# Products of the gated mixer and the joining move from GpSimd to VectorE, reciprocal roots from VectorE to GpSimd, in a one-layer hybrid decoder

## The chip, the cores and the metric

One Trainium2 chip, one of its cores. The metric is the device time of one execution in microseconds; a kernel's time is the median of several runs.

The engines are named PE (TensorE, matrix products), PEld (its loading of the stationary operand), DVE (VectorE), ACT (ScalarE), POOL (GpSimd) and SP (the engine whose queue issues most DMAs). Each engine carries out its instructions in the order in which the program lists them.

## What is computed

One layer over 2048 prompt rows and 64 sample rows (8 sequences of 8), model width 1024:

```
h    = rms_norm(x, g_norm);  proj = h @ w_in           # 1024 -> 3584
u, va, za, q, k, vb, zb = split(proj)
q, k = rms_norm over 64 columns per head (8 heads)
# mixer A, 4 groups of 128 columns, chunks of 128 rows
vn    = rms_norm(va, g_va);  mixed = tril(w_s) @ vn + b_s
a_out = rms_norm(u * mixed, g_oa) * silu(za)
# mixer B: three dilated sliding windows (128/1, 512/4, 2048/16)
for each pattern: o_i, lse_i = softmax attention over its window
b_out = sum_i exp(lse_i) o_i / sum_i exp(lse_i)
b     = rms_norm(b_out, g_ob) * silu(zb)
h     = x + concat(a_out, b) @ w_out
y     = h + sigmoid(h @ w_ple_gate) * rms_norm(p @ w_ple, g_ple)
```

Further outputs are the normed keys, the values and, for the samples, the normed `va`. The samples attend to a cache of 2048 older keys and values.

## The kernel before

Products are made of 16-bit halves (high and low part of each operand, three products), so that every 128-row tile of a weight chunk takes 24 matrix products. The input projection is cut into eight weight chunks, four of kind A (u, va, za of one group, 384 columns) and four of kind B (q, k, vb, zb of two heads, 512 columns), in the order A0 B0 B1 A1 B2 B3 A2 A3. Each chunk runs over 16 prompt tiles and one sample tile; four tiles form a group.

- `xnorm`, `xhalves`, `xtrans` (from line 400) make the normed, split and transposed rows of a tile; the first chunk makes them on its way, so its first products wait for them.
- `b_evac` and `a_evac` copy a product out of PSUM. After each group `b_norm` (line 493) norms q and k, scales the gate and sends it off; `b_trans` splits q and k and has them transposed by DMA into the tile `qk`. `a_norm` (line 573) norms va, and `a_mix` (line 595), some time later, mixes with `w_s`, norms and gates.
- `scores` and `stage_c` are the attention: products into `pss`, maximum and mask on DVE (line 704), exponentials on ACT, split into halves on DVE (lines 715, 716), a DMA that transposes them (`pT`), and products with the values. The patterns' results go to DRAM.
- `combine` (line 755), 16 times, reads three patterns' results of 512 rows and two heads back (`rl`), weights and adds them, norms and gates (`gzl`), and writes to `catd`.
- In the last stage, 17 tiles, `p3_cat`, `p3_out`, `p3_h`, `p3_gate` and `p3_ple` (line 924) make the output products. The samples' attention (`sample`) is spread between them; it multiplies cached keys by queries on POOL (line 1126), and DVE adds these up (line 1127). POOL also adds the residual at the end of each tile (line 963).

`rsqrt` (line 179) is a starting value from the bits and two Newton-like corrections: eight DVE instructions on 1 to 16 columns (lines 183 to 190), called 115 times. Its argument `mul` folds a power of two into the last two steps.

What sets the order: a planner (`Pump`) puts units of attention between the products by costs in nanoseconds written in the code, and a scheduler with a timeline of its own then lays down each engine's list. The list is fixed when the kernel is built.

## Time and profile before

| | |
|---|---|
| median of 3 runs | 1526.22 us (1517.96 to 1528.44) |
| the profiled execution | 1526.24 us, its span 1524.5 us |
| mean granted TensorE clock | 0.959 |
| PE busy | 1361.5 us, 89% of the span, 8280 products |
| DVE busy | 1160.8 us, 76%, 3775 instructions |
| ACT busy | 725.9 us, 48%, 2083 instructions |
| POOL busy | 538.1 us, 35%, 547 instructions |

Busy time is that between start and end of an instruction as recorded; an instruction that started and was held up by something counts as busy. Idle time before an instruction is put down to what ended it. The sum over an engine says little by itself: a stretch in which PE idles and one in which it doesn't are to be read apart.

### The profile page before, as it was taken

To read this page: it belongs to the slowest core of one execution; us is meant where nothing else is said; L and a number is where in the kernel's file an instruction comes from. 1 tells how busy PE (TensorE), PEld (TensorE's weight loads), DVE (VectorE), ACT (ScalarE), POOL (GpSimd) and SP (SyncE) were. 2 spreads that over 40 slices of the span, in tenths; PEclk is the share of its full clock that TensorE was granted. 3 is DMA by queue.
4 is the path that set the end of the run, shared out by engine and by line. 5 is a ranking of instruction groups with operands and counts; after the bars stand their busy time and mean duration, and the time that the engine had idled before them with its cause. 6 is when DMAs were issued, how large, how long until landed. Compare 5 with 4: busy or idle time off the path is not lost. (4 is left out here: it accounts for less than half of the span.)

```text
span 1524.5 us, 26216 instructions
## 1 busy us (share of the span) xinstructions
PE 1361.5 (89%) x8280; PEld 693.3 (45%) x8280; DVE 1160.8 (76%) x3775; ACT 725.9 (48%) x2083; POOL 538.1 (35%) x547
## 2 busy tenths in 40 slices
PE   2989988997899988899888986788998999899998
PEld 1544544554555434455445643443343344344443
DVE  6777887588988789876999899879756675675555
ACT  6675666565656446655665544754322122221222
POOL 7123122234543654322344356643232330330101
PEclk9999999999999999999999998799999999999999
DMA  7983698588965457977697587876899799796432
GB/s 195 238 181 97 131 176 171 119 176 183 210 155 126 132 120 161 215 142 164 151 211 161 127 207 222 230 204 157 208 224 251 188 255 240 194 242 155 105 94 64
DMA packets 591436, 266.06 MB, mean 175 GB/s; under 512 B 338337, under 2 KB 568801, under 8 KB 591297
## 3 DMA queue, kind: packets, MB, share of 16 engines
q1 hardware_dynamic: 589312, 262.73, 75.4%
q0 software_dynamic: 1984, 1.66, 0.7%
q8 instruction: 65, 1.06, 0.3%
q14 instruction: 75, 0.61, 0.1%
HBM read 134.56 MB, written 48.01 MB: 120 GB/s over the span
## 5 line engine op out<-in xcount | busy, mean ns | idle before, releaser
L441 PE MATMUL psg<-wt,xT 128*128 128x512 f16 (+1 forms) x3072 | 649.6, 367 | 36.5 <-DVE agz L571 15.2
L441 PEld LDWEIGHTS <-xT 128*128 128x128 f16 x3072 | 309.9, 102 | 331.3 <-issue 60.1
L712 ACT ACTIVATE sm<-sm,rec,psc 128x256 f32<-128x256 f32 (+1 forms) x384 | 185.1, 546 | 129.4 <-DVE rec L708 103.1
L698 PE MATMUL pss<-qk 128*128 128x256 f16 (+1 forms) x384 | 132.0, 355 | 31.2 <-DMA qk<-qkc 17.2
L1126 POOL TENSOR_TENSOR K<-K,qB 96x512 f32<-96x512 f32 x64 | 88.4, 1386 | 165.8 <-DMA K<-in_cache_k_dram 70.3
L704 DVE CUSTOM_DVE_ANT_0 sm<-pss,mask 128x256 f32<-128x256 f32 (+1 forms) x384 | 122.7, 360 | 29.2 <-PE pss L699 28.1
L699 PE MATMUL pss<-qk 128*128 128x256 f16 (+1 forms) x384 | 132.8, 358 | 0.0
L874 PEld LDWEIGHTS <-Th 128*128 128x128 f16 x800 | 77.1, 99 | 109.9 <-issue 21.5
L874 PEld LDWEIGHTS <-Tc 128*128 128x128 f16 x800 | 76.4, 98 | 110.6 <-issue 19.9
L716 DVE TENSOR_TENSOR pc<-sm,pc 128x512 f16<-128x512 f32 (+1 forms) x160 | 119.0, 744 | 1.6
L963 POOL TENSOR_TENSOR tg<-tg,x 128x1024 f32<-128x1024 f32 (+1 forms) x16 | 37.6, 2347 | 183.4 <-DVE tg L962 160.4
L874 PE MATMUL psg<-w,Th 128*128 128x512 f16 x400 | 97.6, 387 | 1.2 <-DMA Th<-hl 0.5
L861 ACT ACTIVATE hl<-x,sm 128x1024 f16<-128x1024 f32 (+1 forms) x17 | 19.5, 1147 | 166.0 <-DVE sm L842 140.7
L715 DVE CAST pc<-sm 128x512 f16<-128x512 f32 (+1 forms) x160 | 80.5, 503 | 23.3 <-ACT sm L712 21.3
L874 PE MATMUL psg<-w,Tc 128*128 128x512 f16 x400 | 95.6, 379 | 2.8 <-DMA Tc<-hl 2.8
L874 PE MATMUL pss<-w,Th 128*128 128x512 f16 x400 | 94.9, 379 | 0.0
L874 PE MATMUL pss<-w,Tc 128*128 128x512 f16 x400 | 93.8, 379 | 0.0
L1127 DVE TENSOR_REDUCE blk<-K 96x8 f32<-96x512 f32 x64 | 43.0, 678 | 61.2 <-POOL K L1126 61.1
L776 POOL TENSOR_TENSOR rl<-rl,sm 128x520 f32<-128x520 f32 x48 | 55.7, 1187 | 82.9 <-ACT sm L772 80.0
L739 PEld LDWEIGHTS <-pT 128*128 128x128 f16 x600 | 57.3, 98 | 52.7 <-DMA pT<-pc 43.9
L513 POOL TENSOR_TENSOR gz<-gz,gch 128x512 f32<-128x512 f32 x16 | 20.8, 1301 | 168.9 <-DVE gz L491 83.9
L744 ACT ACTIVATE rec<-pso 128x130 f32<-128x130 f32 (+1 forms) x160 | 44.4, 295 | 46.7 <-PE pso L741 45.3
(324 smaller groups left out, 2649.5 us busy)
## 6 DMA issues: line engine op xcount, KB each, us to landing
K<-in_cache_k_dram SPq DMA_DIRECT2D x64, 192.0 KB
qB<-qd SPq DMA_DIRECT2D x64, 192.0 KB
V<-in_cache_v_dram SPq DMA_DIRECT2D x64, 192.0 KB
vt<-vscr SPq DMA_DIRECT2D x32, 258.0 KB
K<-in_cache_k_dram SPq DMA_DIRECT2D x32, 256.0 KB
V<-in_cache_v_dram SPq DMA_DIRECT2D x32, 256.0 KB
cat<-catd SPq DMA_DIRECT2D x16, 512.0 KB
x<-in_x_prompt_dram SPq DMA_DIRECT2D x16, 512.0 KB
```

Source lines behind the costliest of these rows:

```text
L441: last_mm[0] = nc.tensor.matmul(g[:, :ncol], lhsT=l, rhs=r, start=(n == 0), stop=(n == (23 if j < NT else 15)))
L698: nc.tensor.matmul(pss[:, s, h], lhsT=Q[:, h, qs], rhs=KH[:, h, ks], start=True, stop=False)
L699: nc.tensor.matmul(pss[:, s, h], lhsT=Q[:, h, qs], rhs=KL[:, h, ks], start=False, stop=True)
L704: nc.vector.tensor_tensor_reduce(sm4[:, s, h], pss[:, s, h], mk, 1.0, -3.0e38, op0=ALU.add, op1=ALU.max, accum_out=mx[:, i:i + 1])
L712: nc.scalar.activation(sm4[:, s, h], sm4[:, s, h], AF.Exp, bias=r[:, sl + s, h, HD + 1:HD + 2], scale=psc)
L715: nc.vector.tensor_copy(pc[:, :n], smv)
L716: nc.vector.tensor_tensor(pc[:, n:2 * n], smv, pc[:, :n], op=ALU.subtract)
L739: nc.tensor.matmul(po[:, s, h, 0:65], lhsT=H, rhs=v[:, vs_, a:a + 65], start=(bi == 0), stop=False)
L744: nc.scalar.activation(r[:, sl:sl + ns, :, 0:65], po[:, :ns, :, 0:65], AF.Copy)
L776: nc.gpsimd.tensor_tensor(ti, ti, e[:, i, :].unsqueeze(2).to_broadcast([P, 8, 65]), op=ALU.mult)
L874: last_mm[0] = nc.tensor.matmul(gs[hf], lhsT=o[part][:, kt], rhs=w[:, kt % 2, half, :], start=(n[hf] == 0), stop=(n[hf] == (3 if m == P el ...
L1126: nc.gpsimd.tensor_tensor(K3, K3, qB, op=ALU.mult)
```

## The change

Four things are done, and nothing else in the program text:

- `rsqrt` becomes one POOL instruction, a power with the exponent -0.5 out of a constant tile `mhalf`. The powers of two that were folded into the last steps move into the scale and the constant of the instruction ahead, for which `wprep` makes one more column of `sc` (1 DVE instruction in each of the eight chunks).
- In `b_norm`, `a_norm` and `a_mix` the products go from POOL to DVE. In `b_norm` the q half takes row factor and gain in one pass for each head; in `a_mix` the row factor and the gate are one pass for each tile of the group.
- In `combine` the first pattern is scaled on DVE, and the other two are scaled and added in one pass for each of 8 column blocks; the squares go to ACT; row factor and gate are one pass for each block.
- The residual add of the last stage and the key products of the samples stay on POOL.

```diff
-    def rsqrt(src, n, p=P, mul=1.0):
+    def rsqrt(src, n, p=P):
         y = small(n, f"rsy{n}")[:p]
...
-        nc.vector.scalar_tensor_tensor(y, t, 1.5 * 0.375 * mul, y, op0=ALU.add, op1=ALU.mult)
+        nc.gpsimd.tensor_tensor(y, src, mhalf[:p, :n], op=ALU.pow)
         return y
...
@@ b_norm
-        nc.gpsimd.tensor_tensor(rv, rv, y.unsqueeze(2).to_broadcast([m, 4 * n, HD]), op=ALU.mult)
...
-                nc.gpsimd.tensor_tensor(ko[:, q, :].rearrange("p (h d) -> p h d", d=HD), kv[:, q],
+                for h in range(2):
+                    nc.vector.scalar_tensor_tensor(qv[:, q, h], qv[:, q, h], y4[:, q, h:h + 1], gqk,
+                                                   op0=ALU.mult, op1=ALU.mult)
+                nc.vector.tensor_tensor(kv[:, q], kv[:, q], y4[:, q, 2:4].unsqueeze(2).to_broadcast([P, 2, HD]),
+                                        op=ALU.mult)
+                nc.vector.tensor_tensor(ko[:, q, :].rearrange("p (h d) -> p h d", d=HD), kv[:, q],
                                         gkS.unsqueeze(1).to_broadcast([P, 2, HD]), op=ALU.mult)
-                nc.gpsimd.tensor_tensor(qv[:, q], qv[:, q], gqk.unsqueeze(1).to_broadcast([P, 2, HD]), op=ALU.mult)
...
-        nc.gpsimd.tensor_tensor(gzv, gzv, gch[:m, 0, :].unsqueeze(1).to_broadcast([m, n, P]), op=ALU.mult)
+        nc.vector.tensor_tensor(gzv, gzv, gch[:m, 0, :].unsqueeze(1).to_broadcast([m, n, P]), op=ALU.mult)
@@ a_norm
-        nc.gpsimd.tensor_tensor(gz, gz, gch[:m, 0, :].unsqueeze(1).to_broadcast([m, n, P]), op=ALU.mult)
-        nc.gpsimd.tensor_tensor(va, va, y.unsqueeze(2).to_broadcast([m, n, P]), op=ALU.mult)
+        nc.vector.tensor_tensor(gz, gz, gch[:m, 0, :].unsqueeze(1).to_broadcast([m, n, P]), op=ALU.mult)
+        nc.vector.tensor_tensor(va, va, y.unsqueeze(2).to_broadcast([m, n, P]), op=ALU.mult)
@@ a_mix
-        nc.gpsimd.tensor_tensor(t, t, G["gz"][:m, :n, :], op=ALU.mult)
-        nc.gpsimd.tensor_tensor(t, t, y.unsqueeze(2).to_broadcast([m, n, P]), op=ALU.mult)
+        for q in range(n):
+            nc.vector.scalar_tensor_tensor(t[:, q], t[:, q], y[:, q:q + 1], G["gz"][:m, q, :], op0=ALU.mult, op1=ALU.mult)
@@ combine
-        for i in range(3):
-            ti = rr[i][:, :, 0:65]
-            nc.gpsimd.tensor_tensor(ti, ti, e[:, i, :].unsqueeze(2).to_broadcast([P, 8, 65]), op=ALU.mult)
+        nc.vector.tensor_tensor(t0, t0, e[:, 0, :].unsqueeze(2).to_broadcast([P, 8, 65]), op=ALU.mult)
         for i in (1, 2):
-            nc.gpsimd.tensor_tensor(t0, t0, rr[i][:, :, 0:65], op=ALU.add)
+            for a in range(8):
+                nc.vector.scalar_tensor_tensor(t0[:, a], rr[i][:, a, 0:65], e[:, i, a:a + 1], t0[:, a],
+                                               op0=ALU.mult, op1=ALU.add)
...
-        nc.gpsimd.tensor_tensor(sq, o, o, op=ALU.mult)
+        nc.scalar.activation(sq, o, AF.Square)
...
-        nc.gpsimd.tensor_tensor(o, o, y.unsqueeze(2).to_broadcast([P, 8, HD]), op=ALU.mult)
...
-        nc.gpsimd.tensor_tensor(g8, o, g8, op=ALU.mult)
+        for a in range(8):
+            nc.vector.scalar_tensor_tensor(g8[:, a], o[:, a], y[:, a:a + 1], g8[:, a], op0=ALU.mult, op1=ALU.mult)
```

The scheduler makes a new order of all engines from this. Lines of the kernel before and after differ by up to nine; a root is line 181 after. Three places show what moved.

First place, the norm of q and k of the last group of a B chunk. On DVE before, five of the eight steps of a root (lines 185 to 189) stand between the halving of probabilities (715, 716) of the attention:

```order
L185 TENSOR_TENSOR sm_4645<-sm_4645,sm_4642 128x16
L716 TENSOR_TENSOR pc_4580<-sm_4569,pc_4580 128x256
L186 SCALAR_TENSOR_TENSOR sm_4645<-sm_4645 128x16
L187 SCALAR_TENSOR_TENSOR sm_4644<-sm_4645,sm_4644 128x16
L188 TENSOR_TENSOR sm_4645<-sm_4644 128x16
L715 CAST pc_4597<-sm_4586 128x256
L189 SCALAR_TENSOR_TENSOR sm_4645<-sm_4645,sm_4642 128x16
```

After, DVE has the products of the norm there instead (500: q, 502: k), in the midst of maximum (705) and halving (716); the root itself is one row of POOL, whose list holds hardly anything else in this stretch (197 loads a gain):

```order
L705 ISA sm_4252,sm_4253<-pss_4251,mask 128x128
L705 ISA sm_4253 128x1
L716 CAST pc_4243<-sm_4232 128x512
L500 SCALAR_TENSOR_TENSOR raw_4073<-raw_4073,sm_4460,gqk 128x64 x2
L502 TENSOR_TENSOR raw_4073<-raw_4073,sm_4460 128x128
```

```order
L197 DMA gch_3614<-in_g_va_dram 128x128
L181 TENSOR_TENSOR sm_3262<-sm_3260,mhalf 128x16
L181 TENSOR_TENSOR sm_4003<-sm_4001,mhalf 128x16
L181 TENSOR_TENSOR sm_4460<-sm_4458,mhalf 128x16
L181 TENSOR_TENSOR sm_3818<-sm_3814,mhalf 128x8
```

The instruction that makes the power's input (`sm_4458`) stands 17 DVE instructions ahead of the first that reads its result (`sm_4460`).

Second place, the start of POOL's list: loads of gains, of `b_s` (`bsS`) and of pieces of `w_s` (`bd`). Before:

```order
L206 DMA gch_668<-in_g_ob_dram 128x128
L312 DMA bsS<-in_b_s_dram 8x4x1 x8
L317 DMA bd_91<-in_w_s_dram 8x8x1 x4
L292 AFFINE_SELECT w_322<-w_322 128x512
L317 DMA bd_91<-in_w_s_dram 8x8x1 x28
L581 TENSOR_TENSOR agz_331<-agz_331,gch_441 128x512
```

After, the roots of the first input tiles stand between these loads:

```order
L197 DMA gch_567<-in_g_ob_dram 128x128
L305 DMA bsS<-in_b_s_dram 8x4x1 x8
L310 DMA bd_93<-in_w_s_dram 8x8x1 x3
L181 TENSOR_TENSOR sm_158<-sm_155,mhalf 128x1
L285 AFFINE_SELECT w_277<-w_277 128x512
L310 DMA bd_93<-in_w_s_dram 8x8x1 x3
L181 TENSOR_TENSOR sm_185<-sm_182,mhalf 128x1
L310 DMA bd_93<-in_w_s_dram 8x8x1 x17
L181 TENSOR_TENSOR sm_233<-sm_230,mhalf 128x1
```

What was eight DVE instructions for each tile now has loads of constants ahead of it.

Third place, POOL in the last stage, a tile in whose time keys of the samples are multiplied. Before, key products (1126) and the residual add (963):

```order
L1126 TENSOR_TENSOR K_2845_15710<-K_2845_15710,qB_15712 96x512
L1126 TENSOR_TENSOR K_2847_15716<-K_2847_15716,qB_15718 96x512
L963 TENSOR_TENSOR tg_15787<-tg_15787,x_2419_13725 128x1024
L1126 TENSOR_TENSOR K_2851_15737<-K_2851_15737,qB_15739 96x512
L1126 TENSOR_TENSOR K_2853_15743<-K_2853_15743,qB_15745 96x512
L963 TENSOR_TENSOR tg_16079<-tg_16079,x_2380_13561 128x1024
```

After, with the tiles' roots (181):

```order
L1127 TENSOR_TENSOR K_2745_15342<-K_2745_15342,qB_15344 96x512
L964 TENSOR_TENSOR tg_15413<-tg_15413,x_2327_13430 128x1024
L1127 TENSOR_TENSOR K_2749_15363<-K_2749_15363,qB_15365 96x512
L181 TENSOR_TENSOR sm_15478<-sm_15474,mhalf 128x1
L1127 TENSOR_TENSOR K_2751_15369<-K_2751_15369,qB_15371 96x512
L964 TENSOR_TENSOR tg_15697<-tg_15697,x_2291_13288 128x1024
L181 TENSOR_TENSOR sm_15729<-sm_15725,mhalf 128x1
```

A tile's root follows the residual add of the tile ahead, in places with a key product between.

## Rows read from the trace of the kernel before

**Rows 1.** Stretches: us, busy time of each engine, granted clock, DMA share, GB/s.

```profile
0.00:1000.00 1000.00, 866.60 (x5828) 480.37 (x5829) 816.84 (x2902) 584.00 (x1754) 403.58 (x456) 0.95 0.75 170
1000.00:1360.00 360.00, 336.40 (x1663) 142.94 (x1663) 250.42 (x642) 100.74 (x249) 118.11 (x85) 0.98 0.93 215
```

**Rows 2.** Waits of PE: waiter, what ended it, us in total, times, longest.

```profile
PE pso L739 <- DMA pT<-pc: 32.1, 23, 4.3
PE pss L698 <- DMA qk<-qkc: 17.2, 8, 3.6
...
PE psg L441 <- DVE agz L571: 15.2, 6, 6.8
PE pss L698 <- DVE sm L704: 13.6, 16, 1.7
```

**Rows 3.** Groups of DVE: longest and shortest line of the root; busy us, mean ns.

```profile
L184 DVE TENSOR_TENSOR sm<-sm 128x1 f32<-128x1 f32 (+5 forms) x115 | 39.8, 350 | 1.6
...
L188 DVE TENSOR_TENSOR sm<-sm 128x1 f32<-128x1 f32 (+5 forms) x115 | 20.5, 181 | 1.7
```

**Rows 4.** Groups of DVE by form: the nearest to the products that it gets.

```profile
L1147 DVE SCALAR_TENSOR_TENSOR blk<-blk 128x64 f32<-128x64 f32 x4 | 0.9, 220 | 0.0
...
L491 DVE SCALAR_TENSOR_TENSOR gz<-th,psg 128x128 f32<-128x128 f32 x64 | 17.9, 280 | 3.2 <-ACT th L490 3.0
...
L1032 DVE TENSOR_TENSOR blk<-blk,sc 128x512 f32<-128x512 f32 x1 | 0.7, 687 | 0.0
```

**Rows 5.** Timeline at 509 us: start, duration, instruction, idle before it.

```profile
509.03 1.44 DVE L184 TENSOR_TENSOR sm<-sm 64x1 f32<-64x1 f32 x1
...
509.42 1.03 POOL L781 TENSOR_TENSOR rl<-rl 128x512 f32<-128x512 f32 x1
```

**Rows 6.** Groups of DVE, two by form, two by line.

```profile
L716 DVE TENSOR_TENSOR pc<-sm,pc 128x512 f16<-128x512 f32 x140 | 108.5, 775 | 1.4
...
L715 DVE CAST pc<-sm 128x512 f16<-128x512 f32 x140 | 71.6, 511 | 22.6 <-ACT sm L712 20.7 <-DMA pT<-pc 0.9 <-DMA kd<-sb 0.2
...
L708 DVE TENSOR_SCALAR rec<-sm,nsc 128x2 f32<-128x2 f32 (+1 forms) x160 | 54.5, 353 | 10.4 <-DMA r2d<-rec 5.9 <-DMA r3d<-rec 2.4 <-DMA r1d<-rec 1.7
...
L617 DVE TENSOR_SCALAR sm<-sm,sm 128x4 f32<-128x4 f32 (+1 forms) x20 | 19.5, 975 | 11.1 <-ACT ua L615 8.4 <-ACT sb L615 2.7
```

**Rows 7.** Timeline of DVE at 656 us.

```profile
656.34 0.22 DVE L708 TENSOR_SCALAR rec<-sm,nsc 128x2 f32<-128x2 f32 x1
656.47 0.42 DVE L715 CAST pc<-sm 128x512 f16<-128x512 f32 x1
656.92 0.69 DVE L716 TENSOR_TENSOR pc<-sm,pc 128x512 f16<-128x512 f32 x1
```

**Rows 8.** PE at 651 us, and the stretch behind it (columns of rows 1).

```profile
651.08 0.39 PE L698 MATMUL pss<-qk 128*128 128x256 f16 x1 [3.54 <-DMA qk<-qkc]
...
651.90:654.70 2.80, 2.80 (x9) 1.08 (x8) 2.55 (x12) 0.15 (x1) 0.00 (x0) 0.60 0.57 115
```

**Rows 9.** Groups of POOL: a small product, the shortest iota, the longest product.

```profile
L511 POOL TENSOR_TENSOR sb<-sb,gqS 64x128 f32<-64x128 f32 x4 | 1.8, 444 | 0.0
...
L1057 POOL IOTA blk<- 128x2 int32 x1 | 0.1, 129 | 0.5 <-DVE sc L1054 0.5
...
L963 POOL TENSOR_TENSOR tg<-tg,x 128x1024 f32<-128x1024 f32 (+1 forms) x16 | 37.6, 2347 | 183.4 <-DVE tg L962 160.4 <-DVE sm L184 21.1 <-DVE sm L937 1.9
```

**Rows 10.** Timeline of the start.

```profile
13.21 1.13 ACT L416 ACTIVATE xhl<-room,sm 128x1024 f16<-128x1024 f32 x1
...
13.82 1.62 POOL L312 DMA_DIRECT2D bsS<-in_b_s_dram  x3 [1.70 <-DMA gch<-in_g_oa_dram]
...
22.34 5.90 PE L441 MATMUL psg<-wt,xT 128*128 128x384 f16 x24 [4.58 <-DMA xT<-xhl]
```

**Rows 11.** Waits: POOL from 1060 to 1365 us; DVE over the span.

```profile
POOL K L1126 <- DMA K<-in_cache_k_dram: 66.2, 12, 22.3
...
DVE blk L1127 <- POOL K L1126: 61.1, 30, 7.7
```

More of the change, by code (lines that the diff above doesn't have):

```diff
@@ L213, in tile_hymba_gmlp_dilated_attn_step @@
     nc.scalar.activation(small(1), ones[:, 0:1], AF.Square)
+    mhalf = cst.tile([P, 16], F32, name="mhalf")
+    nc.gpsimd.memset(mhalf, -0.5)
     mask = cst.tile([P, 2, P], BF16, name="mask")
@@ L374, in wprep @@
         nc.vector.tensor_scalar(sc[:, 4:5], sc[:, 3:4], VS * VS, None, op0=ALU.mult)
+        nc.vector.tensor_scalar(sc[:, 5:6], sc[:, 3:4], 2.0 ** -24, None, op0=ALU.mult)
         yield 0.0
@@ L406, in xnorm @@
             xsq[j] = nc.scalar.activation(hl[:m, 1].bitcast(BF16), xt[:m], AF.Square, accum_out=s2[:m])
-            nc.vector.tensor_scalar(s2[:m], s2[:m], 1.0 / D, EPS, op0=ALU.mult, op1=ALU.add)
-            y = rsqrt(s2[:m], 1, m, XS)
+            nc.vector.tensor_scalar(s2[:m], s2[:m], XS ** -2 / D, XS ** -2 * EPS, op0=ALU.mult, op1=ALU.add)
+            y = rsqrt(s2[:m], 1, m)
         xhl[j] = hl, y
@@ L496, in b_norm @@
         ms = small(16, "bms", 2)
-        nc.vector.tensor_scalar(ms[:m, :4 * n], G["ss"][:m, :4 * n], 1.0 / HD, sc[:m, 3:4], op0=ALU.mult, op1=ALU.add)
-        y = rsqrt(ms[:m, :4 * n], 4 * n, m, 2.0 ** 12)
-        rv = G["raw"][:m, :n, :].rearrange("p j (a d) -> p (j a) d", d=HD)
-        nc.gpsimd.tensor_tensor(rv, rv, y.unsqueeze(2).to_broadcast([m, 4 * n, HD]), op=ALU.mult)
+        nc.vector.tensor_scalar(ms[:m, :4 * n], G["ss"][:m, :4 * n], 2.0 ** -24 / HD, sc[:m, 5:6], op0=ALU.mult, op1=ALU.add)
+        y = rsqrt(ms[:m, :4 * n], 4 * n, m)
+        y4 = y.rearrange("p (j a) -> p j a", a=4)
         kv = G["raw"][:m, :n, 128:256].rearrange("p j (h d) -> p j h d", d=HD)
@@ L505, in b_norm @@
             for q in range(n):
-                nc.gpsimd.tensor_tensor(ko[:, q, :].rearrange("p (h d) -> p h d", d=HD), kv[:, q],
+                for h in range(2):
[4 more added lines that the diff above has]
+                nc.vector.tensor_tensor(ko[:, q, :].rearrange("p (h d) -> p h d", d=HD), kv[:, q],
                                         gkS.unsqueeze(1).to_broadcast([P, 2, HD]), op=ALU.mult)
-                nc.gpsimd.tensor_tensor(qv[:, q], qv[:, q], gqk.unsqueeze(1).to_broadcast([P, 2, HD]), op=ALU.mult)
         else:
-            nc.gpsimd.tensor_tensor(kv[:, 0], kv[:, 0], gkS[:m].unsqueeze(1).to_broadcast([m, 2, HD]), op=ALU.mult)
-            nc.gpsimd.tensor_tensor(qv[:, 0], qv[:, 0], gqS[:m].unsqueeze(1).to_broadcast([m, 2, HD]), op=ALU.mult)
+            for h in range(2):
+                nc.vector.scalar_tensor_tensor(qv[:, 0, h], qv[:, 0, h], y4[:, 0, h:h + 1], gqS[:m],
+                                               op0=ALU.mult, op1=ALU.mult)
+                nc.vector.scalar_tensor_tensor(kv[:, 0, h], kv[:, 0, h], y4[:, 0, h + 2:h + 3], gkS[:m],
+                                               op0=ALU.mult, op1=ALU.mult)
         gzv = G["gz"][:m, :n, :]
-        nc.gpsimd.tensor_tensor(gzv, gzv, gch[:m, 0, :].unsqueeze(1).to_broadcast([m, n, P]), op=ALU.mult)
+        nc.vector.tensor_tensor(gzv, gzv, gch[:m, 0, :].unsqueeze(1).to_broadcast([m, n, P]), op=ALU.mult)
         if m == P:
@@ L937, in p3_ple @@
         nc.vector.tensor_tensor(ms[:m], s2[:m, 0:1], s2[:m, 1:2], op=ALU.add)
-        nc.vector.tensor_scalar(ms[:m], ms[:m], 1.0 / D, None, op0=ALU.mult)
-        nc.vector.scalar_tensor_tensor(ms[:m], ic[:m], EPS, ms[:m], op0=ALU.mult, op1=ALU.add)
-        y = rsqrt(ms[:m], 1, m, 0.5)
+        nc.vector.tensor_scalar(ms[:m], ms[:m], 4.0 / D, None, op0=ALU.mult)
+        nc.vector.scalar_tensor_tensor(ms[:m], ic[:m], 4.0 * EPS, ms[:m], op0=ALU.mult, op1=ALU.add)
+        y = rsqrt(ms[:m], 1, m)
         e = wk.tile([P, D], F32, name=nm("e"), tag="raw", bufs=2)
```

13 lines of the change are left out of this document (3 added, 10 removed).

## Prediction

> **What bounds the kernel now.** I read the stretches first, then TensorE's waits, then the groups of VectorE and GpSimd. In the first 1000 us [rows 1] TensorE is busy 866.6 us and idle 133.4; VectorE is busy 816.8, GpSimd 403.6, and the granted clock averages 0.95. In the next 360 us TensorE is busy 336.4, so 23.6 idle: that later stage is TensorE's own work, and nothing that VectorE saves there comes back as time. What can be won lies in the 133.4 us. The waits of TensorE [rows 2] name who ends them: the transposed probabilities pT 32.1 us, the transposed q and k halves 17.2, the gate evacuation of the mixer 15.2, the row maximum that frees score banks 13.6, together 78.1. The first two are put down to a DMA, but what each DMA carries (pc, qkc) is written by VectorE just before. So VectorE, with 183.2 us free in 1000, is what feeds TensorE late; ScalarE and the queue of SP stand beside it in the same chains.
>
> **What goes from VectorE.** A root is eight instructions, called 115 times. Its eight lines are eight groups, of which [rows 3] show the longest (39.8 us) and the shortest (20.5); the eight together are 228.0 us.
>
> **What comes to VectorE.** Durations [rows 4]: 0.220 us for a scaled product of 128x64, 0.280 for 128x128 (its second operand is in PSUM, the nearest row), 0.687 for a plain product of 128x512.
> - Norm of q and k, 16 groups: eight products of 64 columns, eight of 128, one of 512: 1.76 + 2.24 + 0.69 = 4.69, in all 75.0 us.
> - Mixer norm, 16 groups: two of 512, 22.0 us. Mixer end: four of 128, 17.9 us.
> - Joining, 16 times: one of 520 columns (taken as 0.687), 16 of 65 and eight of 64 (taken as 0.220): 5.97, in all 95.5 us.
> - The sample groups: 16 small q and k products, 8 plain gate and value products, 4 gate products and 4 joint ones at 0.22 to 0.28: 7.9 us.
>
> Sum 218.3, so VectorE's own work falls by 9.7 us only. The squares of the joining go to ScalarE, 16 instructions; that engine was busy 584.0 of 1000 [rows 1], which hides them; uncovered they would cost some 11 us (estimate: 16 at the 0.687 us of a 512-column product [rows 4]).
>
> **What VectorE gets back from GpSimd.** [rows 5] show the price of the old placing: a 64x1 step of the root took 1.44 us and ended with the GpSimd product that ran beside it (509.42 + 1.03). The same lengthening stands in the means [rows 6] against the same lines while GpSimd is quiet [rows 7]: the 512-column difference 775 against 690 ns, 140 times, 11.9 us; the cast 511 against 420, 140 times, 12.7; the bias 353 against 220, 160 times, 21.3; the mixer's mean square 975 against the same 220 for a short tensor-scalar, 20 times, 15.1. That is 61.0 us. Smaller groups are left uncounted, and the products of the sample keys and of the final sum stay on GpSimd, so the last stage keeps its collisions. VectorE in all: -9.7 - 61.0 = -70.7 us, nearly all of it in the first 1000 us: 746 busy, 254 free.
>
> **From VectorE to TensorE.** An instruction's wait in a line behind others grows roughly as busy over free time: 816.8/183.2 = 4.46 before, 746/254 = 2.94 after, a third less. I apply that third (34%) to the 78.1 us of [rows 2]: -26.6 us. The bounds are none of them (the chains may hang on DMA and ScalarE alone) and all of them, -78.1. The removed GpSimd steps themselves also shorten the way from the norm to the transposed q and k; this is in the same 17.2 us and not counted again.
>
> [...]
>
> **The power.** No row shows one. The nearest GpSimd instruction by shape [rows 9] is a 64x128 product at 0.444 us; the shortest, an iota of two elements, takes 0.129; the longest product 2.347. I take 0.444, near the low end because a root has 1 to 16 elements, and keep 0.129 to 2.347 for the range. The eight steps it replaces take 228.0/115 = 1.98 us, so at 0.444 the value comes sooner. In the built order 38 of the 115 powers have at most two VectorE instructions between the instruction that makes their input and the one that reads the result, and 15 have none; the other 77 are covered by attention's instructions. At 0.444 us no wait is left that counts.
>
> **The start.** GpSimd's queue is strict, and the first power now stands behind its eight small loads of b_s and three of w_s [second order place]. Those loads issue until 15.44 us, three more at 0.54 (1.62 us for three) end at 17.06 [rows 10], so the first root comes at about 17.5 us, where ScalarE used it at 13.21. The first transposed tile is then up to 4.3 us later, and TensorE began its first product at 22.34 having waited for just that. It idles again a few us later for the second tile, which takes up part: +2 us, bounds 0 and 4.3. [...]
>
> **The last stage.** There each tile's root stands behind a GpSimd product of the final sum, for some tiles behind products of sample keys too [third order place], and these wait for their loads: 66.2 us in 12 waits, the longest 22.3 [rows 11]. VectorE reads those products in its own strict order and waited 61.1 us for them already, while TensorE idled only 23.6 us in 360. I charge +5 us; bounds 0 and 23.6 (as much idling again).
>
> **Sum**, against the profiled 1526.24 us, which equals the median 1526.22: -26.6 - 10 + 2 + 5 = -29.6, so 1496.6, rounded 1497.
>
> **Rivals.**
> - *The waits stay.* 49.3 of the 78.1 us are written against DMAs, and a transposed DMA, its place in SP's queue and ScalarE's exponentials keep their length. A VectorE that is freer then waits itself. For it: the order is fixed in advance. Against it: 28.8 us are put down to VectorE directly. Nothing gained, +7: about 1526 with the start and the last stage partly hidden.
> - *The power is dear, the slow side.* One mechanism: VectorE, strict in order, stands at the reader of a root until GpSimd is done. The relief of 70.7 us is used up when the 115 roots cost 0.61 us of standing each; from there it turns. At 0.8 us each VectorE loses 92, is 21 us worse than before, at 838 of 1000; 838/162 = 5.17 is 16% above 4.46, so +12.5 on the waits, +5 on the clock, +7: 1551. For it: no row has the power, and 38 roots stand nearly bare. Against it: 1 to 16 elements, and 77 covered; the bare ones alone would need 1.9 us of standing each.
> - *The whole wait goes.* All 78.1 and 29 of the clock, +7: 1426. The order of all engines is made anew, which can help or hurt. For it only the size of the relief on GpSimd (403.6 us of 1000); against it the DMAs.
>
> **How the numbers follow.** Forecast 0.55 (its own range 1475 to 1513), waits stay 0.20, dear power 0.20, all gone 0.05. A measurement of this kernel can tell about 1% (15 us). Faster by more than that: most of the forecast, 0.51, and the last rival, 0.05: 0.56. Slower: the dear power and a part of the rest whose loss at the start or in the last stage reaches its bound, 0.24. The same: 0.20. The low end of the range takes two thirds of the four waits and their share of the clock, -52 - 20 + 2 + 5, 1461, and a little of the all-gone case: 1455. The high end takes most of the dear power: 1545.
>
> **What would show it.** Right: VectorE's busy time near 1090 us, its short lines at their quiet lengths (the bias near 220 ns), the four waits of TensorE near 52 us together, the granted clock of the first 1000 us at 0.96 or more, powers below 0.5 us each. Wrong: VectorE waiting for the power's line in its list of waits for tens of us; the four waits as before although VectorE is freer; a first product of TensorE later than 27 us; idle TensorE in the last stage.

## The result, and the profile after

The changed kernel takes 1534.57 us (median of 20 runs, 1526.64 to 1541.69), the kernel before 1524.22 us in the 20 runs beside it. The ratio is 1.0071, 95% interval 1.0054 to 1.0089: 10 us slower, not 29 us faster. Its profiled execution has a span of 1532.7 us and a mean granted clock of 0.942 (before: 1524.5 us, 0.959).

The busy times of the page: VectorE fell by 100.7 us, GpSimd by 220.8, TensorE is within 5 us of where it was (1365.9 against 1361.5).

```profile
PE 1365.9 (89%) x8280; PEld 695.6 (45%) x8280; DVE 1060.1 (69%) x3663; ACT 736.1 (48%) x2099; POOL 317.3 (21%) x279
```

The two stretches of [rows 1], same columns (us; busy time of PE, PEld, DVE, ACT, POOL; granted clock; DMA share; GB/s):

```profile
0.00:1000.00 1000.00, 863.80 (x5781) 477.73 (x5782) 738.51 (x2935) 579.34 (x1725) 186.49 (x185) 0.92 0.75 165
1000.00:1360.00 360.00, 334.90 (x1672) 143.97 (x1671) 233.78 (x547) 114.12 (x292) 108.96 (x79) 0.97 0.94 221
```

In the first 1000 us VectorE is busy 738.5 us where 746 was forecast and 816.8 stood before. TensorE should have done more there; it is busy 863.8, before 866.6, at a clock of 0.92 instead of 0.95.

VectorE's groups that answer to [rows 6], by line (busy us, mean ns of one | idle before it):

```profile
L717 DVE TENSOR_TENSOR pc<-sm,pc 128x512 f16<-128x512 f32 (+1 forms) x160 | 104.8, 655 | 1.2
...
L716 DVE CAST pc<-sm 128x512 f16<-128x512 f32 (+1 forms) x160 | 65.1, 407 | 27.0 <-ACT sm L713 26.5
...
L709 DVE TENSOR_SCALAR rec<-sm,nsc 128x2 f32<-128x2 f32 (+1 forms) x160 | 34.7, 226 | 23.2 <-DMA r3d<-rec 13.6 <-DMA r2d<-rec 8.3 <-DMA r1d<-rec 0.9
...
L618 DVE TENSOR_SCALAR sm<-sm,sm 128x4 f32<-128x4 f32 (+1 forms) x20 | 4.4, 221 | 8.1 <-ACT ua L616 7.5 <-ACT sb L616 0.5
```

The bias went from 353 to 226 ns, the mean square from 975 to 221, the cast (all forms) from 503 to 407, the difference (all forms) from 744 to 655. The relief came as worked out.

TensorE's waits that answer to [rows 2] (us in total, times, longest):

```profile
PE pso L740 <- DMA pT<-pc: 53.7, 32, 5.8
PE psg L435 <- DMA xT<-xhl: 23.1, 8, 8.9
...
PE pss L699 <- DVE sm L705: 12.7, 9, 3.8
...
PE psg L435 <- DVE agz L571: 6.0, 5, 2.1
PE pss L699 <- DMA qk<-qkc: 3.8, 1, 3.8
```

The four of [rows 2] were 78.1 us; they are 53.7 + 3.8 + 6.0 + 12.7 = 76.2. The wait for q and k and that for the gate are nearly gone, that for the transposed probabilities grew from 32.1 to 53.7, and the input rows `xT` stand for 23.1.

The powers by form (columns as above, mean ns second):

```profile
L181 POOL TENSOR_TENSOR sm<-sm,mhalf 128x16 f32<-128x16 f32 x16 | 48.5, 3030 | 334.0 <-DVE sm L491 276.4 <-DVE sm L361 32.0 <-DVE v L466 25.6
...
L181 POOL TENSOR_TENSOR sm<-sm,mhalf 128x4 f32<-128x4 f32 x32 | 36.6, 1148 | 170.5 <-DVE sm L618 106.5 <-DVE sm L578 42.5 <-DVE rec L709 21.5
...
L181 POOL TENSOR_TENSOR sm<-sm,mhalf 128x8 f32<-128x8 f32 x16 | 30.8, 1923 | 157.9 <-DVE sm L788 146.1 <-DVE sm L843 11.6
...
L181 POOL TENSOR_TENSOR sm<-sm,mhalf 128x1 f32<-128x1 f32 x37 | 24.3, 658 | 69.3 <-DVE sm L401 41.6 <-DVE sm L940 22.5 <-DVE sm L1222 4.8
```

A power takes 658 ns on one column and 3030 on sixteen; the mean of all 115 is 1.336 us. Yet VectorE stood little for them; its two longest waits for a root are:

```profile
DVE e L945 <- POOL sm L181: 8.4, 13, 0.7
...
DVE sm L620 <- POOL sm L181: 3.7, 7, 0.9
```

The start, timeline (start, duration, instruction, idle before it):

```profile
17.57 0.59 POOL L181 TENSOR_TENSOR sm<-sm,mhalf 128x1 f32<-128x1 f32 x1
...
21.50 5.74 POOL L310 DMA_DIRECT2D bd<-in_w_s_dram  x10
...
26.53 6.38 PE L435 MATMUL psg<-wt,xT 128*128 128x384 f16 x24 [3.21 <-DMA xT<-xhl]
...
48.87 1.46 PE L435 MATMUL psg<-wt,xT 128*128 128x384 f16 x4 [8.93 <-DMA xT<-xhl]
```

The first power runs at 17.57 us, as forecast, and TensorE's first product at 26.53 instead of 22.34 [rows 10]: 4.2 us later, nearly the upper bound of 4.3. The second tile starts at 35.87 us, 0.7 later than before (35.19); for the third TensorE waits 8.93 us. At the sample tile, which ends the first chunk, the changed kernel is 8.4 us late (117.9 against 109.5 us).

Where the time went is seen by cutting the first 800 us of both traces:

```profile
0.00:100.00 100.00, 63.33 (x345) 35.99 (x346) 72.46 (x293) 65.66 (x154) 41.81 (x69) 0.93 0.97 217
100.00:700.00 600.00, 547.82 (x3716) 297.23 (x3715) 483.18 (x1765) 345.34 (x1054) 216.30 (x244) 0.95 0.70 153
700.00:800.00 100.00, 88.23 (x654) 48.94 (x653) 87.41 (x304) 63.27 (x189) 39.72 (x44) 0.97 0.84 179
```

That is the kernel before; the changed kernel:

```profile
0.00:100.00 100.00, 55.86 (x296) 30.95 (x297) 43.75 (x110) 60.18 (x136) 42.70 (x80) 0.95 0.85 199
100.00:700.00 600.00, 557.09 (x3753) 301.46 (x3752) 467.58 (x1950) 353.27 (x1077) 82.05 (x50) 0.95 0.72 154
700.00:800.00 100.00, 74.70 (x553) 41.86 (x551) 72.83 (x327) 53.23 (x152) 8.26 (x4) 0.80 0.76 163
```

TensorE's busy time gained 9.3 us between 100 and 700, and lost 7.5 at the start and 13.5 between 700 and 800. The last projection product starts at 1032.5 us instead of 1018.0, 14.5 later, of which 8.4 were there at the end of the first chunk; from it to the end the kernel takes 500.2 us instead of 506.5. Between 700 and 800 the changed kernel has a gap without any projection product; all instructions first, then the projection's line alone (PE, PEld, clock, DMA share, GB/s):

```profile
746.00:784.00 38.00, 16.03 (x146) 10.57 (x147) 31.71 (x141) 20.94 (x57) 1.88 (x1) 0.53 0.72 158
```

```profile
746.00:784.00 38.00, 0.00 (x0) 0.12 (x1) 0.53 0.72 158
```

Before, the projection alone kept TensorE busy for 24.0 of these 38 us, at a clock of 0.96. Now TensorE had only attention; it was busy 16.0 us, and the granted clock was 0.53.

### The profile page after: what moved, and what is told of

It reads as the page before. It is cut to its first block, busy times and chain, and to the rows that moved or that the text cites. A ratio compares the mean times of both kernels' runs of the same rounds, so it can differ in the third digit from the quotient of the medians.

```text
span 1532.7 us, 25743 instructions
## 1 busy us (share of the span) xinstructions
PE 1365.9 (89%) x8280; PEld 695.6 (45%) x8280; DVE 1060.1 (69%) x3663; ACT 736.1 (48%) x2099; POOL 317.3 (21%) x279
## 3 DMA queue, kind: packets, MB, share of 16 engines
q0 software_dynamic: 1984, 1.66, 0.8%
## 4 chain that ended last, share of the span: by engine, by line
PE 50%; DMA 18%; DVE 15%; ACT 5%; SPq 5%; issue 4%; POOL 1%; POOLq 0%; DVEq 0%; ACTq 0%
PE psg L435 20%; PE psg L875 8%; PE pss L875 8%; PE pss L699 3%; PE pss L700 3%; DMA pT<-pc 3%; DMA qB<-qd 2%; SPq L419 2%; DMA K<-in_cache_k_dram 2%; DVE rl L778 2%; PE pso L1207 2%; DVE sm L705 1%; PE pso L1112 1%; ACT sm L713 1%; DMA rl<-r3d 1%
## 5 line engine op out<-in xcount | busy, mean ns | idle before, releaser
L435 PE MATMUL psg<-wt,xT 128*128 128x512 f16 (+1 forms) x3072 | 651.0, 368 | 32.4 <-DMA xT<-xhl 23.1
L181 POOL TENSOR_TENSOR sm<-sm,mhalf 128x1 f32<-128x1 f32 (+5 forms) x115 | 153.2, 1336 | 830.9 <-DVE sm L491 318.2
L699 PE MATMUL pss<-qk 128*128 128x256 f16 (+1 forms) x384 | 133.5, 359 | 16.6 <-DVE sm L705 12.7
L700 PE MATMUL pss<-qk 128*128 128x256 f16 (+1 forms) x384 | 134.8, 363 | 0.0
L717 DVE TENSOR_TENSOR pc<-sm,pc 128x512 f16<-128x512 f32 (+1 forms) x160 | 104.8, 655 | 1.2
L716 DVE CAST pc<-sm 128x512 f16<-128x512 f32 (+1 forms) x160 | 65.1, 407 | 27.0 <-ACT sm L713 26.5
L740 PE MATMUL pso<-vt,pT 128*128 128x65 f16 x352 | 42.6, 197 | 24.7 <-DMA pT<-pc 22.8
```

The lines of the kernel that those rows point to most:

```text
L181: nc.gpsimd.tensor_tensor(y, src, mhalf[:p, :n], op=ALU.pow)
L435: last_mm[0] = nc.tensor.matmul(g[:, :ncol], lhsT=l, rhs=r, start=(n == 0), stop=(n == (23 if j < NT else 15)))
L699: nc.tensor.matmul(pss[:, s, h], lhsT=Q[:, h, qs], rhs=KH[:, h, ks], start=True, stop=False)
L700: nc.tensor.matmul(pss[:, s, h], lhsT=Q[:, h, qs], rhs=KL[:, h, ks], start=False, stop=True)
L716: nc.vector.tensor_copy(pc[:, :n], smv)
L717: nc.vector.tensor_tensor(pc[:, n:2 * n], smv, pc[:, :n], op=ALU.subtract)
```

## The experiments

Three theories were open at first: the start, the powers, and the products on VectorE. The first four runs undo a part each; every kernel's order is remade by the scheduler.

**All roots back**, in the 115 calls the eight VectorE instructions of before.

```diff
-        nc.gpsimd.tensor_tensor(y, src, mhalf[:p, :n], op=ALU.pow)
+        nc.vector.tensor_scalar(y.bitcast(I32), src.bitcast(I32), -0.5, MAGIC, op0=ALU.mult, op1=ALU.add)
...
+        nc.vector.scalar_tensor_tensor(y, t, 1.5 * 0.375, y, op0=ALU.add, op1=ALU.mult)
```

> All 115 roots go back to eight VectorE steps, the products stay on VectorE. Start theory (powers of the third and fourth tile stand behind the small loads in GpSimd's queue): the third tile's product no longer waits 8.9 us, first product near 22.3 us, time about 1524, 10 us below the changed kernel's 1534.6. Joining theory (25 VectorE instructions of the joining in one row hold up the score chain): VectorE gets 228 us more to do, the pT waits stay near 54 us or grow, time 1535 or more. Power theory (1.3 us a root, 3.0 at 16 columns, is what costs): 1524 or below.

Measured: 1534.36 us, ratio to before 1.0054 (1.0036 to 1.0072). The gap remains (TensorE busy 75.7 us between 700 and 800). Taken together, the powers are not what makes the change slow; single groups of them may still cost or save, and the last runs take these apart.

**The start's roots back** (17 roots of the input norm on VectorE; `newton` is the old eight steps).

```diff
-            y = rsqrt(s2[:m], 1, m)
+            y = newton(s2[:m], 1, m)
```

> Only the 17 roots of the input norm go back to eight VectorE steps; the other 98 stay powers. Start theory: the third tile's wait of 8.9 us goes, time 1524 to 1527. Joining theory: pT waits stay near 54 us and the time falls by no more than 3, to about 1532. Power theory (roots of 4 to 16 columns): no more than 2 below 1534.6.

Measured: 1535.41 us, 1.0062 (1.0038 to 1.0086). The start is as before (63.8 us busy in the first 100), and the last projection product starts at 1019.7 us instead of 1032.5. But from it to the end the kernel takes 511.4 us instead of 500.2: the gain is given back in the last stage, in which the edit changes nothing but the order.

**Joining back on GpSimd.**

```diff
-        nc.vector.tensor_tensor(t0, t0, e[:, 0, :].unsqueeze(2).to_broadcast([P, 8, 65]), op=ALU.mult)
+        for i in range(3):
+            ti = rr[i][:, :, 0:65]
+            nc.gpsimd.tensor_tensor(ti, ti, e[:, i, :].unsqueeze(2).to_broadcast([P, 8, 65]), op=ALU.mult)
```

> Only the products of the joining (and its squares) go back to GpSimd, roots stay powers, norms and mixers stay on VectorE. Joining theory: pT waits back to 32 to 40 us, TensorE's busy time between 700 and 800 us back from 75 to 85 or more, time 1520 to 1526. Start theory: the first 100 us as in the changed kernel (55.9 busy), time 1532 to 1536. [...]

Measured: 1533.79 us, 1.0054 (1.0033 to 1.0075); busy 81.3 us between 700 and 800. Half of the gap is filled, and the total does not move.

**All products back, powers alone.**

```diff
-                nc.vector.tensor_tensor(kv[:, q], kv[:, q], y4[:, q, 2:4].unsqueeze(2).to_broadcast([P, 2, HD]),
-                                        op=ALU.mult)
...
+                nc.gpsimd.tensor_tensor(qv[:, q], qv[:, q], gqk.unsqueeze(1).to_broadcast([P, 2, HD]), op=ALU.mult)
```

> All products go back to GpSimd as in the kernel before, all roots are powers. Joining theory: faster than the kernel before where the 228 us of root steps are gone, 1510 to 1520, or at least not slower. Start theory: first 100 us lose about 8 us as in the changed kernel, time 1530 to 1536 unless the freed VectorE makes up for it. Power theory: powers now stand behind GpSimd's products as well, 1535 to 1550.

Measured: 1535.07 us, 1.0064 (1.0042 to 1.0086). The stretch from 700 to 800, all engines:

```profile
700.00:800.00 100.00, 90.05 (x640) 49.20 (x638) 70.51 (x263) 56.33 (x166) 42.32 (x37) 0.96 0.79 163
```

No gap, at a clock of 0.96, and still as slow. So the gap comes with the products, and filling it does not bring the time back. From the last projection product to the end the kernel takes 517.1 us here (before 506.5), in an execution of 1543.2 us, 8 above the median. That the powers lengthen the last stage is not shown by this: two kernels below take 515 us there as well, one without any power (the neutral change, 515.0, whose last projection product starts at 1010.0 us) and one without a power in the last stage (1538.57 us, 515.9).

**Three mixtures**, to find out which products and which powers: joining alone on VectorE (norms and mixers on GpSimd, input roots old); all products on GpSimd with powers only where neither the start nor the last stage reads them; norms and mixers on VectorE with the joining on GpSimd and input roots old. Their edits are the pieces above, combined.

> Roots of the input norm by eight VectorE steps, the products of the norms of q and k and of the mixers back on GpSimd; the joining stays on VectorE, the other roots stay powers. Order theory (with the norms' products on VectorE TensorE's order spends its projection products during one pair's attention and has none beside the start of the next): TensorE always has projection products, busy 86 us or more between 700 and 800 us, time 1518 to 1526. Joining theory: the stretch without projection products stays (busy 70 to 77 between 700 and 800), time 1532 to 1536.

> All products on GpSimd as in the kernel before; powers only in the norms of q and k, mixers, joining and samples (66 roots), eight VectorE steps for the input norm and the last stage. Start and last-stage theory (the 1535 of powers alone came from 10 us at the start and 8 us in the last stage): first product at 22 to 23 us, last stage 500 us, time 1512 to 1520, faster than the kernel before. Power theory (each power costs where it stands in the norms): 1530 or more. Order scatter (any change of the order loses what the kernel before had by its order): 1526 to 1536.

> Roots of the input norm by eight VectorE steps, the joining's products back on GpSimd; norms of q and k and mixers stay on VectorE, other roots powers. Order theory: a stretch without projection products of 25 us or more between 740 and 790, busy 75 to 82 between 700 and 800, time 1526 to 1534. Joining theory: no such stretch, 1518 to 1524.

Measured: 1541.3 us, 1.0100 (1.0075 to 1.0124); 1538.57 us, 1.0078 (1.0057 to 1.0099); 1531.57 us, 1.0041 (1.0022 to 1.0061). The first misses both of its ranges; the second (81 powers by its trace, not the 66 that its expectation counts) has the time that was given to the power theory; the third lies in the range of its order theory. No sum of parts explains these numbers, so the order itself came under suspicion.

**A neutral change**: before, and one VectorE instruction of 128x1 in each of the eight chunks whose result nobody reads.

```diff
+            nc.vector.tensor_scalar(sc[:, 5:6], sc[:, 3:4], 2.0 ** -24, None, op0=ALU.mult)
```

> The kernel before with one more VectorE step of one column in the preparation of each of the eight weight chunks, its result read by nobody; TensorE's products stand in another order in 932 of 7921 places. It costs some 1 us of VectorE. Order scatter: 3 to 10 us off the kernel before in either direction. If the order matters little: within 3 us.

Measured: 1529.71 us, 1.0022 (1.0005 to 1.0038). Eight small instructions move 932 TensorE products to other places and cost 3 us. That is how far the remade order alone scatters, in the one sample taken.

**The order held.** In two kernels each of 8032 of TensorE's products got an edge of issue order, without a semaphore, to the one that follows it in the other kernel: the change in the order of before, and before in the order of the change.

```diff
+    for a, b in zip(row, row[1:]):
+        tc.add_manual_dep(ins[b], ins[a].name, mybir.DependencyInfo(
+            mybir.DependencyClass.NoSync, mybir.DependencyReason.DATA), reason="order")
```

> The changed kernel, with TensorE's 8032 products held to the order in which the kernel before issues them (edges of issue order alone, no wait on a semaphore added). Order theory (the change's gain is lost by TensorE's re-made order): the stretch without projection products near 744 us is gone, busy between 700 and 800 back to 86 or more; the third tile's wait at the start remains, some 9 us; time 1512 to 1524. Start and row theory (what costs is the powers and the long rows of VectorE steps themselves): 1530 to 1540, the waits for pT stay above 45 us.

> The kernel before, with TensorE's products held to the order in which the changed kernel issues them. Order theory: the stretch without projection products appears here too, busy between 700 and 800 falls from 88 to 75 to 80, time 1532 to 1545. If the powers and the rows are what costs: within 3 us of the kernel before.

Measured: 1542.6 us, 1.0115 (1.0086 to 1.0143), and 1574.75 us, 1.0328 (1.0293 to 1.0363). An order fits the durations it was made for: the remade one is 8 us better for the change, and 49 us worse for before. So the loss is not a mishap of TensorE's new order; with TensorE's list unchanged it is larger. But a held order has a price of its own, as the 49 us show, and both kernels lie above every range expected. A loss in a held run is therefore the change's and the misfit's together.

**The same, with two of the variants** (input roots old; powers without start and last stage). As the list of TensorE is now that of before, the traces can be laid beside each other stretch by stretch.

> The changed kernel with the 17 roots of the input norm back on VectorE, and TensorE's products held to the order of the kernel before. Order theory: start as before (third tile without a 9 us wait) and no stretch without projection products, so what is left is the relief of VectorE: time 1500 to 1515. Start and row theory: 1525 to 1535.

> All products on GpSimd, powers only in norms, mixers, joining and samples (as in the run that has powers in the middle alone, 1538.6), and TensorE's products held to the order of the kernel before. Order theory: 1515 to 1526, as little order is left to differ and VectorE does less. Power theory (the power's length in the chain of the norm costs): 1532 to 1540.

Measured: 1547.83 us, 1.0151 (1.0124 to 1.0179), and 1543.53 us, 1.0127 (1.0100 to 1.0154). Both lie above all their ranges again. Three stretches of before, cut at products of TensorE (all engines):

```profile
345.07:420.69 75.62, 62.12 (x500) 36.18 (x498) 68.68 (x248) 45.18 (x136) 34.60 (x39) 0.93 0.90 195
420.69:500.00 79.31, 76.48 (x556) 46.93 (x556) 65.42 (x249) 44.42 (x146) 33.40 (x27) 0.94 0.60 141
740.11:820.02 79.91, 71.06 (x566) 41.42 (x565) 72.97 (x249) 46.95 (x146) 40.12 (x44) 0.98 0.88 188
```

The same products with the change, order held, input roots old:

```profile
341.39:433.25 91.86, 68.52 (x501) 38.16 (x499) 79.21 (x344) 47.88 (x141) 14.46 (x9) 0.83 0.87 187
433.25:507.60 74.35, 74.35 (x557) 46.10 (x557) 47.82 (x185) 43.18 (x141) 6.05 (x6) 0.95 0.54 114
751.98:855.42 103.44, 80.57 (x566) 44.34 (x565) 85.77 (x374) 51.14 (x156) 17.36 (x10) 0.85 0.87 176
```

The first and third are the crowded ones, where the joining of one pair of heads meets the norm of the next one. Before, VectorE had 75.62 - 68.68 = 6.9 us free in the one and 6.9 in the other. The change brings it 10.5 and 12.8 us more work there; the stretches grow by 16.2 and 23.5 us and the clock falls to 0.83 and 0.85. In the second stretch VectorE does 17.6 us less, and 5.0 us come out of it. The whole span grew by 17.5 us: 39.8 lost at two places, 22.3 gained over all others. Whether the added work is the cause is tested by the other held kernel of this pair, whose products all stay on GpSimd:

```profile
341.19:427.83 86.64, 68.17 (x500) 38.25 (x498) 67.83 (x206) 46.06 (x140) 52.67 (x52) 0.85 0.92 181
745.35:829.69 84.34, 73.13 (x566) 42.74 (x565) 65.55 (x214) 47.45 (x147) 54.13 (x54) 0.94 0.85 182
```

VectorE has 18.8 us free in each, and yet the first stretch is 11.0 us longer than before, the third only 4.4. So the loss of the third needs VectorE's added work; much of the first is there without it. TensorE's waits in the first stretch, change (order held, input roots old) and then before:

```profile
PE pss L715 <- DVE sm L721: 18.7, 10, 5.0
PE pso L756 <- DMA pT<-pc: 4.6, 3, 2.8
```

```profile
PE pso L739 <- DMA pT<-pc: 7.1, 4, 2.7
PE pss L698 <- DVE sm L704: 3.6, 4, 1.7
```

VectorE's list there, with the change (start, duration, idle before it):

```profile
345.86 0.41 DVE L721 CUSTOM_DVE_ANT_0 sm<-pss,mask 128x256 f32<-128x256 f32 x1
...
348.54 0.29 DVE L732 CAST pc<-sm 128x256 f16<-128x256 f32 x1 [2.06 <-ACT sm L729]
348.74 0.28 DVE L520 TENSOR_TENSOR ko<-raw,gkS 128x128 f32<-128x128 f32 x1
348.95 0.28 DVE L563 TENSOR_TENSOR qkc<-raw,qkc 128x128 f16<-128x128 f32 x1
...
349.69 0.16 DVE L804 SCALAR_TENSOR_TENSOR sm<-sm,sm 128x8 f32<-128x8 f32 x1
...
351.16 0.22 DVE L725 TENSOR_SCALAR rec<-sm,nsc 128x2 f32<-128x2 f32 x1
```

Between the row maximum (721) at 345.86 us and the next bias (725) at 351.16 stand, after a wait for ScalarE, products of the norm (520), halvings of q and k (563, 564) and steps of the joining (804, 784). TensorE's wait for the maxima is 18.7 us in this stretch, before 3.6.

**The split.** If the crowded stretches are the cause, the change only outside of them should gain, and the change only in them should lose. "Outside" means: mixers, norm of pair 1, joining of pair 4, last stage and samples as in the change; input roots, joining of pairs 1 to 3 and norms of pairs 2 to 4 as before.

```diff
+JOIN_POOL = (0, 1, 2)
+NORM_POOL = (1, 2, 3)
...
+        y = (newton if hp in NORM_POOL else rsqrt)(ms[:m, :4 * n], 4 * n, m)
+        if hp in NORM_POOL:
+            nc.gpsimd.tensor_tensor(rv, rv, y.unsqueeze(2).to_broadcast([m, 4 * n, HD]), op=ALU.mult)
```

> TensorE's order held to that of the kernel before. The changed code only where VectorE has room: mixers, norm of the first head pair, joining of the last, last stage and samples; the code of before for the input norm's roots, for the joining of the first three pairs and for the norms of the last three. Peak theory (VectorE is the bound from 345 to 420 and from 740 to 820 us, where a pair's joining meets the next pair's norms; the change adds 10 to 13 us of VectorE there and takes some 30 us off elsewhere): those two stretches as before, time 1500 to 1518. Power theory or a misfit of the held order: 1532 to 1545, as the three other held runs.

> TensorE's order held. The reverse: the changed code, with its powers, only in the joining of the first three pairs and the norms of the last three; the code of before everywhere else. Peak theory: the 16, 9 and 23 us lost in those stretches stay lost and the gains of the others go, time 1545 to 1575. If the peaks are not what costs: below 1540.

Measured, order held: 1539.49 us, 1.0090 (1.0072 to 1.0108), and 1551.58 us, 1.0155 (1.0132 to 1.0178). The first and third stretch, outside only:

```profile
345.92:441.55 95.63, 65.35 (x501) 37.96 (x499) 74.73 (x264) 46.85 (x141) 46.84 (x50) 0.81 0.83 175
760.02:844.16 84.14, 74.77 (x567) 42.70 (x566) 74.95 (x262) 49.26 (x153) 39.67 (x43) 0.94 0.87 185
```

At the crowded places only:

```profile
347.71:438.27 90.56, 67.95 (x499) 37.95 (x498) 78.43 (x348) 48.07 (x140) 14.41 (x10) 0.85 0.85 187
750.33:851.49 101.16, 79.22 (x567) 44.44 (x566) 84.92 (x374) 51.57 (x155) 18.74 (x11) 0.87 0.87 175
```

The second run came as expected: 14.9 and 21.3 us lost, nearly what the whole change loses. The first missed the range of the peak theory and fell into the one given to powers or a misfit of the held order. Its third stretch is mended (4.2 us longer than before), its first is not (20.0 longer), although VectorE has 20.9 us free there; TensorE stands once, for the sample tile:

```profile
PE psg L453 <- DVE fold L465: 13.8, 1, 13.8
```

This wait is a misfit of the lists, not a VectorE without room. ScalarE's copy of the sample rows ended at 395.1 us; its DMA (464) stands in SP's list behind transposes and other transfers and was issued at 409.98; VectorE's addition (465) came at 416.73, behind two casts and two differences that took 1.12 to 1.66 us each beside GpSimd's products of the joining, where they had taken 0.42 and 0.69 at 404 us. So over the held kernels the third stretch bears out that the added work costs the time: it is 17.2 (the change), 23.5 and 21.3 us longer with it, 4.4 and 4.2 without. The first stretch, 11.0 and 20.0 us longer without that work, does not.

**The split with an order of its own**, alone and with 22 more roots returned (last stage 17, samples 4, one in the gain's preparation).

```diff
-        y = rsqrt(ms[:m], 1, m)
+        y = newton(ms[:m], 1, m)
-        y = rsqrt(den, 1)
+        y = newton(den, 1)
```

> The same split as in the held one, TensorE's order left to be made anew. Peak theory: 1500 to 1520, faster than the kernel before or the same. Order scatter alone: 1528 to 1538.

> The split, order made anew, and with the roots of the last stage, of the samples and of the one gain preparation on VectorE too, so that 36 of 115 roots are powers. Peak theory: within 5 us of the split with the powers there, 1500 to 1520; if the powers of the last stage cost: some 5 us less than that one. Order scatter alone: 1528 to 1538.

Measured: 1521.67 us, 0.9970 (0.9951 to 0.9988), and 1515.17 us, 0.9916 (0.9890 to 0.9942). Both beat both kernels, the first just outside its range. The stretch from 700 to 800 in the split:

```profile
700.00:800.00 100.00, 88.33 (x637) 48.83 (x636) 83.04 (x298) 60.41 (x178) 40.41 (x44) 0.92 0.79 173
```

TensorE is busy 88.3 us again in these 100. The better one keeps 49 powers (not the 36 that its expectation counts) and leaves VectorE 1119.0 us of work by its page, more than the change did.

**Which powers.** The split with every root on VectorE, and the whole change with the input's 17 and these 22 returned, so that all products stay on VectorE.

> The products split as in the two runs before, all 115 roots by eight VectorE steps. If the 36 powers left in the best run so far (1515.2) help there by taking steps off VectorE: 1518 to 1524. If powers are at best neutral: 1510 to 1517.

> The changed kernel, all its products on VectorE, with the roots of the input norm, the last stage, the samples and the gain preparation on VectorE, so that powers stay in norms, mixers and joining. If the powers of the last stage cost 5 to 7 us, as the split runs let expect (1521.7 against 1515.2): 1528 to 1531, against 1535.4 of the run with the input norm's roots alone. If they cost nothing there: 1534 to 1537. Either way above the split by the price of the peaks, 12 us or more.

Measured: 1532.67 us, 1.0054 (1.0031 to 1.0077), and 1519.09 us, 0.9943 (0.9917 to 0.9969). Both miss: the first lies above its ranges, the second below, and it is only 3.9 us above the split with the same roots returned, where 12 or more were expected for the crowded places. The intervals of these two overlap (0.9917 to 0.9969, 0.9890 to 0.9942). Yet this kernel has all products on VectorE and still has the gap:

```profile
700.00:800.00 100.00, 74.61 (x539) 41.33 (x537) 74.68 (x330) 55.64 (x161) 9.42 (x4) 0.79 0.80 166
```

It is faster than before with the gap, and the runs at 1535.07 and 1538.57 us are slower without it (TensorE busy 90.05 and 92.52 us there). So neither the gap nor the work at the crowded places decides the time once the order is remade.

As differences of medians, the 49 powers of the split (mixers 40, norm 5, joining 4) save 17.5 us (1532.67 - 1515.17), the 76 left in the whole change 15.3 us (1534.36 - 1519.09), and the 22 late ones cost 16.3 us there (1535.41 - 1519.09) and 6.5 in the split. Each of these pairs differs in its order too, so how much is the powers' own is not shown. Waits from 1020 us on, with these 22 as powers:

```profile
DVE blk L1141 <- POOL K L1140: 74.4, 35, 9.5
PE pst L1120 <- ACT KT L1130: 13.1, 3, 5.0
```

and as VectorE steps:

```profile
DVE blk L1141 <- POOL K L1140: 60.3, 28, 6.8
PE pst L1120 <- ACT KT L1130: 4.9, 4, 2.5
```

With the powers gone from among the products of the sample keys (lines 1140 and 1141 here), VectorE waits 14.1 us less for these, TensorE 8.2 less for the banks of the transposes, and from the last projection product to the end it is 497.0 us instead of 511.4 (in the split 500.4 instead of 509.5). The powers are not the only source of such waits: the kernel of 1538.57 us, without a power in the last stage, has 67.3 and 15.3 us of the same two.

One wait follows the products through every remade order, whatever is done with the roots: TensorE's for the transposed probabilities, over the whole span.

| products on VectorE | kernels | wait for `pT`, us |
|---|---|---|
| all (the change; all, 17 or 39 roots returned) | 4 | 53.7; 52.4, 55.9, 55.5 |
| joining alone; norms and mixers alone | 3 | 43.5; 49.1, 44.1 |
| only outside the crowded places (three splits) | 3 | 31.9, 24.6, 35.4 |
| none (before, neutral, two with powers) | 4 | 32.1, 28.7, 28.8, 37.5 |

Of the 53.7 us, 14.0 fall into the 38 us of the gap, where before has 2.8. The time does not follow this wait one for one: 55.5 and 24.6 us belong to the two kernels that are 3.9 us apart.

## Why the prediction was wrong

- **VectorE's work** (-70.7 us): right in its mechanism, too small over the whole span, -100.7. The new products are 225.1 us where 218.3 were summed; the relief of the other instructions is some 98 us (100.7 + 225.1 - 228.0), where 61.0 were counted and smaller groups left out. In the first 1000 us it is 738.5 against 746, and the short lines have the lengths forecast.
- **From VectorE to TensorE** (-26.6 us): this is the step that failed. "An instruction's wait in a line behind others grows roughly as busy over free time [...] I apply that third (34%)", the author's estimate, turns free time, averaged over 1000 us, into shorter waits. The free time came (261.5 us, forecast 254), the shorter waits did not: the four are 76.2 us of 78.1, where 52 were forecast. Those for q and k and for the gate fell by 22.6 us, the one for the transposed probabilities grew by 21.6, and it grew so in all four kernels with these products on VectorE: what VectorE was freed of shortened some waits, and what it was given lengthened another. Even with the start's roots returned, TensorE has 5836 products behind it at 1000 us, before 5828. One place where the added work costs more than the average says is shown with TensorE's order held, the stretch from 740 us: 6.9 us free before, 12.8 more work, 23.5 us longer, and 4 longer without that work.
- **The clock** (-10 us in the sum, +5 and 29 in the rivals, 20 in the range): the author's estimate, and no run shows these terms; [rows 8] have one short stretch at a low clock, not what a wait costs over 1000 us. The runs showed the other sign: the granted clock is 0.92 over the first 1000 us, before 0.95, with TensorE idle for 136.2 us of them, before 133.4, and it is 0.53 in the gap.
- **The power** (0.444 us): too low by a factor of three on average (1.336). The slow rival's own mechanism is not what happened in the change: VectorE stood 8.4 + 3.7 us at readers of a root, not 70. That "no wait is left that counts" nearly holds all the same is luck in the price: the instructions in between cover the longer power too.
- **The start** (+2 us): mis-sized. The first tile is 4.2 us late, and the third tile's 8.93 us wait was not seen, because only the first power's place behind the loads was counted, not the 17 further loads of `w_s`; the first chunk ends 8.4 us late. Over the whole run nothing of it is left to measure: with these roots returned the time is the same. The first power has no delay of its own: the load ahead ends at 17.56 us, the power starts at 17.57 and takes 0.59 us.
- **The last stage** (+5 us, bound 23.6): in the changed kernel the time from the last projection product to the end is 6.3 us shorter than before, so the charge found nothing there. Against the same kernel with the late roots on VectorE the price is 16.3 us (start's roots returned too) or 6.5 (split); with all products on GpSimd, returning the 17 of the last stage and the input's gave nothing (1538.57 against 1535.07). It hangs on the rest of the order.
- **The forecast "waits stay"** comes nearest in form, 76.2 of 78.1 us, but by waits that grew against waits that fell, not because VectorE's relief reaches none of them.

Shown: VectorE's relief came and TensorE's four waits did not shrink with it, because the moved products lengthen the wait for the transposed probabilities, in every order tried; and, with TensorE's products in the same order, one crowded place where work added to VectorE costs more time than it takes. Not settled: how the 10 us of the change are made up. In remade orders the split is worth 14 us with the late powers (1535.41 to 1521.67) and 4 without them (1519.09 to 1515.17), the second not clear of noise; the neutral change scatters by 3, in one sample; and the mixtures at 1541.3 and 1538.57 have no account. For the times, an order scatter of the size of these differences is the rival that is left.

## What to carry to other kernels

Free time averaged over a long stretch is no measure of how much shorter another engine's waits become: here the average of 18% free hid two places with 9%, and the waits as a whole stayed. Before moving work, cut the trace into windows and look at the receiving engine's free time where the work lands; then test the place by the same stretch without that work, since one of the two lost time either way. Such a change can also be made in part: returning 39 of the 115 roots gave 1519.09 us where the whole change gave 1534.57, and moving fewer products besides gave 1515.17, a further 4 us that are not clear of noise. And where a scheduler remakes the order, two kernels differ by their order as well as by the edit: hold the order of the engine that sets the end to compare stretch by stretch, and remember that a held order that fits badly costs time of its own.
